# Modulation chunks held back by a tile in the first layer's first expert product, 32 of them from tile 24 on, and eight moved to the second layer's

## The chip, the cores and the metric

The kernel runs on one core of a Trainium2 chip. The metric is device time in microseconds (us) of one execution; the time before is 1799.27 us, the median of 3 runs from 1798.03 to 1800.52 us.

## The reference

A decoder trunk of two layers on 256 tokens of width 1024, all in float32. What matters here is the modulation by a conditioning vector `c`, of which each layer needs six groups of 1024 numbers, and the expert stage (PEER):

```python
mod = (c_act @ w_ada + b_ada)[:, None, :]
sh1, sc1, g1, sh2, sc2, g2 = jnp.split(mod, 6, axis=-1)
h = rms_norm(x, norm1_g) * (1 + sc1) + sh1
...
x = x + g1 * (merged @ w_out)
h2 = rms_norm(x, norm2_g) * (1 + sc2) + sh2
x = x + g2 * peer_ffn(h2, peer_wq, peer_sub_keys, peer_down, peer_up)
```

In `peer_ffn` each token picks 16 of 16384 experts for each of 8 heads, and computes the sum of `gate * gelu(h2 . down[expert]) * up[expert]`.

## The kernel before, in words

The kernel computes the expert stage densely: a **first product** of all 256 tokens with all of `down`, in 128 tiles of 128 experts, then gelu and a mask of gates, then a **second product** with `up`, again in 128 tiles. The matrices stream from HBM in transfers of 512 KB (128 x 1024 float32).

The work before an expert stage (mixing, queries, scores) is the same in both layers. Two stretches between stages, the bridges, apply the updates and the norm.

**The stream.** `Src.seq` lists every matrix of the program in order. `dma_ahead` (line 170) issues their transfers on SP's queue into a ring of 5 buffers, `raw`; a transfer waits until the buffer's last reader is done. `cast_step` (line 207) takes the next entry. A matrix is split for TensorE into `hi` (line 232, ACT) and `lo` (line 225, DVE), 3 buffers each, at raised priority, so that two tiles stand ready ahead of the one that PE multiplies. `chunk_mm` multiplies a tile: 8 times the three matmuls of lines 303 to 305.

**Modulation chunks.** 128 of the modulation's numbers take one 512 KB transfer of `w_ada` and a multiply with a sum on DVE (`ada_chunk`, lines 188 to 205). They are mixed into the stream. `ada(layer, groups)` lists them by groups of 8 chunks, and `mix(a, b, first, last)` spreads the chunks `b` over the entries `first` to `last` of `a`. In the first layer's first product there are 40: its own last group and four of the second layer's. In that product the conditioning vector stands in two PSUM banks, and a chunk is two instructions of 512 columns each (line 193): one sums into `mod`, one into `halves`. Its second product has 16 more, with the vector in SBUF (`cb`). The second layer's products have none.

**Between the tiles.** In the first third of a first product DVE still does the top-k work of the retrieval (`run_fill`). Then the gates come in, four tokens at a time: POOL makes one-hots (line 918, 4 an item), DVE others (lines 921 and 923), PE multiplies them, and DVE multiplies the gates into the activations (`gate_use`, line 939), for the columns that are there; ACT copies the others (line 942). `act_use` (line 971) multiplies gelu values in. Each second tile, ACT writes `ungated` values to HBM (lines 949 and 950), and SP copies rows of `up` (line 951).

A scheduler with a cost model of its own sets the order in which the instructions stand on each engine, within priorities; on the chip each engine then takes its instructions in that order and waits at each for what it needs. `tc.keep_in_program_order(op)` adds an edge of order: the instruction stays behind the one of its engine that was written just before it.

Of the kernel before, what the change touches and what calls it, by code (L numbers as in the profile page):

```python
# [9 lines left out]
F32 = mybir.dt.float32  # L10
# [4 lines left out]
OP = mybir.AluOpType  # L15
# [43 lines left out]
def hybrid_trunk(ctx: ExitStack, tc: tile.TileContext, x_in, c_in, vec_in, w_ada, w_in, w_out, w_pq,  # L59
# [103 lines left out]
    class Src:  # L163
# [2 lines left out]
        loaded = 0  # L166
        cast = 0
        seq = []

    def dma_ahead(upto):  # L170
        while Src.loaded < min(upto, len(Src.seq)):
# [16 lines left out]
    def ada_chunk(layer, col, raw):  # L188
        sides = Src.c if isinstance(Src.c, list) else [Src.c]
        w = D // len(sides)  # L190
        for k, (c, m) in enumerate(zip(sides, (mods[layer], halves))):
            v = raw[:, k * w:(k + 1) * w]
            nc.vector.scalar_tensor_tensor(v, v, 1.0, c, op0=OP.mult, op1=OP.mult, accum_out=m[:, col:col + 1])  # L193
        n = 8
        if layer == 0 and col < G1:
            n = 1
        if (col + 1) % n == 0:
            lo = col + 1 - n
            m = mods[layer][:, lo:lo + n]
            if len(sides) > 1:  # L200
                nc.vector.tensor_add(m, m, halves[:, lo:lo + n])
            nc.vector.tensor_add(m, m, vec[:, layer, V_ADA + lo:V_ADA + lo + n])
            if lo // 8 in (SC1 // 8, SC2 // 8):
                at = lo % 8 + (V_N1 if lo // 8 == SC1 // 8 else V_N2)
                nc.vector.scalar_tensor_tensor(m, m, 1.0, vec[:, layer, at:at + n], op0=OP.add, op1=OP.mult)

    def cast_step(late=None):
        k = Src.cast
        if k >= len(Src.seq):
            return False  # L210
        dma_ahead(k + 1)
        kind, _, arg = Src.seq[k]
        raw = raws.pop(k)
        Src.cast += 1
        if kind == "ada":
            ada_chunk(arg[0], arg[1], raw)
        elif kind in ("whole", "early"):
            ready.append((raw, None))
        else:
            hi = stream.tile([P, D], F32R, name="hi", tag="hi", bufs=3)  # L220
            lo = stream.tile([P, D], F32R, name="lo", tag="lo", bufs=3)

            def low():
                if arg is None:
                    nc.vector.tensor_sub(lo, raw, hi.bitcast(F32))  # L225
                else:
                    nc.vector.scalar_tensor_tensor(lo, raw, arg, hi.bitcast(F32), op0=OP.mult,
                                                   op1=OP.subtract)

            with tc.high_priority(offset=AHEAD):  # L230
                if arg is None:
                    nc.scalar.copy(hi, raw)  # L232
                else:
                    nc.scalar.activation(hi, raw, AF.Copy, scale=arg)
                if late is None:
                    low()
                else:
                    late.append(low)
            ready.append((hi, lo))
        dma_ahead(k + RAW)  # L240
        return True

# [12 lines left out]
    def ada(layer, groups):  # L255
        return [("ada", w_ada[layer, p], (layer, p)) for g in groups for p in range(8 * g, 8 * g + 8)]
# [15 lines left out]
    for layer in range(DEPTH):  # L272
# [15 lines left out]
        dn = mats(down, layer, 128)  # L288
        ups = [("whole" if n // 2 in WHOLE_UP[layer] else "mat", up[layer, n], None) for n in range(128)]
        if layer + 1 < DEPTH:  # L290
            dn = mix(dn, ada(0, [5]) + ada(1, range(4)), 4, 112)
            ups = mix(ups, ada(1, [4, 5]), 6, 120)
        seq += dn + ups
    Src.seq = seq
    dma_ahead(RAW)
# [610 lines left out]
    def experts(layer, rest):  # L906
# [195 lines left out]
                turn(1, 1, high)  # L1102
            return low + high, qg

        if layer + 1 < DEPTH:
            Src.c = [bank("acc", 4) for _ in range(2)]
            for k, half in enumerate(Src.c):
                nc.scalar.copy(half, cact[:, k * 512:(k + 1) * 512])
        gdone = 0
        made = 0  # L1110
        waiting = []
# [138 lines left out]
```

## Time and profile before

| | |
|---|---|
| median of 3 runs | 1799.27 us |
| profiled execution | 1804.13 us, span 1802.4 us |
| first layer's first product, tile 0 to tile 127 | 188.67 to 617.31 us |
| second layer's first product, tile 0 to tile 127 | 1092.32 to 1488.19 us |
| DVE's waits for chunk transfers, whole span | 57.3 us |

The stages are told apart by counting the matmuls of line 303: 8 for each tile. The profile shows, for a stretch, how long each engine was busy, and for each wait what ended it. Engines issue in order, so an instruction that waits holds all that stands behind it on its engine.

### The profile page before, as it was taken

Reading aid. Unit: us, or ns where it says so; the run is one execution under the profiler, and the core shown is the slowest. Engines: PE = TensorE matmul, PEld = TensorE weight load, DVE = VectorE, ACT = ScalarE, POOL = GpSimd, SP = SyncE. Lnnn points to the kernel's source line nnn. Section 1 sums busy time; section 2 is a strip of 40 time slices with the busy share of each in tenths; the row PEclk is TensorE's granted clock in tenths of the full one; section 3 lists DMA queues with packets and bytes.
Section 4 is the critical chain, followed back from the end, with each engine's and each line's share of the span. In section 5 each row is a group of like instructions: output and inputs, shape, how many; then the busy total and the mean of one; then the engine's idle time right before and its main releaser. Section 6 shows DMA issues by size and latency. Waiting matters only on the chain. (4 is left out here: it accounts for less than half of the span.)

```text
span 1802.4 us, 34404 instructions
## 1 busy us (share of the span) xinstructions
PE 1736.8 (96%) x12504; PEld 1599.5 (89%) x12504; DVE 1515.8 (84%) x3465; ACT 913.6 (51%) x1419; POOL 907.5 (50%) x826
## 2 busy tenths in 40 slices
PE   7999999999999999999999999999999999999998
PEld 6789899998988988888889999999999998888886
DVE  5858998878888789999987589967778877999998
ACT  2446455544444554445556664555555546444543
POOL 1000101577879556657620002037999973777672
PEclk9999999999999999999999999999999999999999
DMA  9965798888887789999974456988787778999995
GB/s 366 312 231 173 227 299 287 280 254 269 268 257 247 237 313 328 334 346 344 341 255 141 146 171 212 294 287 247 248 255 245 237 234 283 360 354 349 350 351 206
DMA packets 189867, 492.83 MB, mean 273 GB/s; under 512 B 19521, under 2 KB 85441, under 8 KB 188546
## 3 DMA queue, kind: packets, MB, share of 16 engines
q1 hardware_dynamic: 134752, 405.33, 67.4%
q0 software_dynamic: 19984, 68.44, 10.4%
q10 hardware_dynamic: 34962, 16.88, 3.2%
q8 instruction: 98, 1.61, 0.4%
q14 instruction: 71, 0.58, 0.1%
HBM read 470.64 MB, written 61.87 MB: 295 GB/s over the span
## 5 line engine op out<-in xcount | busy, mean ns | idle before, releaser
L232 ACT CAST hi<-raw 128x1024 fp32r<-128x1024 f32 x538 | 564.5, 1050 | 616.7 <-PE ch L305 265.9
L225 DVE TENSOR_TENSOR lo<-raw,hi 128x1024 fp32r<-128x1024 f32 x538 | 660.4, 1228 | 118.6 <-ACT hi L232 117.1
L304 PE MATMUL ch<-hh,lo 128*128 128x256 f32 x2336 | 655.2, 281 | 15.5 <-DVE lo L225 15.5
L303 PE MATMUL ch<-hh,hi 128*128 128x256 f32 x2336 | 660.3, 283 | 5.9 <-ACT ungated L949 5.8
L305 PE MATMUL ch<-hh,hi 128*128 128x256 f32 x2336 | 651.6, 279 | 0.0
L918 POOL TENSOR_SCALAR oh<-iota,picks 128x128 f16<-128x128 f16 x512 | 498.4, 991 | 235.4 <-DVE arena L833 67.4
L1008 POOL DMA_INDIRECT arena<-rows,arena x256 | 371.2, 1450 | 221.1 <-DVE arena L1019 113.3
L304 PEld LDWEIGHTS ch<-hh,lo 128*128 128x128 f32 x2336 | 443.5, 190 | 18.8 <-DVE lo L225 18.4
L303 PEld LDWEIGHTS ch<-hh,hi 128*128 128x128 f32 x2336 | 441.9, 189 | 7.1 <-ACT ungated L949 6.6
L305 PEld LDWEIGHTS ch<-hh,hi 128*128 128x128 f32 x2336 | 441.8, 189 | 0.0
L1028 PE MATMUL acc<-hi,hh 128*128 128x512 f32 (+2 forms) x1920 | 419.5, 359 | 2.8 <-DVE hh L986 2.4
L1028 PEld LDWEIGHTS acc<-hi,hh 128*128 128x128 f32 x1920 | 339.4, 188 | 49.3 <-DVE hh L986 6.4
L1028 PE MATMUL acc<-lo,hh 128*128 128x512 f32 x960 | 230.9, 361 | 2.8 <-DVE lo L225 2.7
L1028 PEld LDWEIGHTS acc<-lo,hh 128*128 128x128 f32 x960 | 172.7, 188 | 27.7 <-DVE lo L225 5.1
L1019 DVE SCALAR_TENSOR_TENSOR arena<-arena 128x256 f32<-128x256 f32 (+1 forms) x254 | 140.2, 552 | 9.1
L942 ACT ACTIVATE arena<-g 128x240 f32<-128x240 f32 (+35 forms) x128 | 41.5, 324 | 117.0 <-DVE arena L939 108.1
L779 POOL CAST arena<-arena 128x512 f16<-128x512 uint32 x32 | 26.3, 835 | 147.7 <-DVE arena L768 119.2
L923 DVE TENSOR_TENSOR oh<-oh,parts 128x512 f16<-128x512 f16 x256 | 99.9, 432 | 0.0
L193 DVE SCALAR_TENSOR_TENSOR raw<-raw,acc 128x512 f32<-128x512 f32 x80 | 51.8, 683 | 47.8 <-DMA raw<-in_w_ada 47.8
L931 PE MATMUL g<-oh 128*128 128x128 f16 x512 | 76.3, 222 | 13.9 <-POOL oh L918 9.6
L1014 DVE SCALAR_TENSOR_TENSOR arena<-arena,chosen,ident 128x128 f32<-128x128 f32 x256 | 88.6, 346 | 0.0
L921 DVE TENSOR_TENSOR oh<-iota,parts 128x512 f16<-128x512 f16 x128 | 56.6, 443 | 27.5 <-POOL oh L918 15.0
(231 smaller groups left out, 1788.4 us busy)
## 6 DMA issues: line engine op xcount, KB each, us to landing
raw<-in_down SPq DMA_DIRECT2D x256, 512.0 KB, 4.4
raw<-in_up SPq DMA_DIRECT2D x256, 512.0 KB, 5.2
raw<-in_w_ada SPq DMA_DIRECT2D x96, 512.0 KB, 5.1
rows<-in_up SPq DMA_DIRECT2D x64, 384.0 KB, 5.1
raw<-in_w_pq SPq DMA_DIRECT2D x32, 512.0 KB, 3.7
rows<-in_up SPq DMA_DIRECT2D x64, 256.0 KB, 5.1
rows<-ungated ACTq DMA_DIRECT2D x128, 128.0 KB, 4.5
raw<-in_w_in SPq DMA_DIRECT2D x26, 512.0 KB, 4.4
```

Source lines behind the costliest of these rows:

```text
L225: nc.vector.tensor_sub(lo, raw, hi.bitcast(F32))
L232: nc.scalar.copy(hi, raw)
L303: nc.tensor.matmul(dst, hi[:, cols], k[0], start=start, stop=False, **kw)
L304: nc.tensor.matmul(dst, lo[:, cols], k[0], start=False, stop=False, **kw)
L305: nc.tensor.matmul(dst, hi[:, cols], k[1], start=False, stop=stop, **kw)
L918: nc.gpsimd.tensor_scalar(oh[:, i, :], iota, picks[:, t:t + 1], None, op0=OP.is_equal)
L923: nc.vector.tensor_tensor(og[j], on, wide(1 + j), op=OP.mult)
L931: nc.tensor.matmul(dst, oh[:, i, :], og[0][:, i // 2, :, i % 2], start=True, stop=False)
L1008: nc.gpsimd.indirect_dma_start(out=ring[:, k % RING, :], out_offset=None, in_=rows[layer][:, :], in_offset=bass.IndirectOffsetOnAxis(ap=wh ...
L1014: nc.vector.scalar_tensor_tensor(v[:, wide:], v[:, wide:], chosen[:, 1, k:k + 1], ident, op0=OP.mult, op1=OP.mult, accum_out=w8[:, k:k + 1])
L1019: nc.vector.scalar_tensor_tensor(total, v[:, :wide], w8[:, k:k + 1], total, op0=OP.mult, op1=OP.add)
L1028: nc.tensor.matmul(acc[piece][:, :hi - lo], w[:, t * P:(t + 1) * P], u[:, lo:hi], start=piece not in opened, stop=last, skip_group_check=True)
```

## The change

Four edits:

- In `cast_step` a chunk that comes while the vector is in PSUM isn't computed at once. It is put into `Src.held`, and computed when the next matrix has been split.
- The first half of each such chunk (into `mod`) is kept in program order, that is behind that split's `lo`. The second half (into `halves`) is not.
- The first layer's first product gets 32 chunks, spread from tile 24 to 124, instead of 40 from tile 4 to 112. One group of eight, group 5 of the second layer, moves to the second layer's first product, tiles 40 to 120. The second product keeps 16 (groups 3 and 4 instead of 4 and 5).
- For that, the second layer loads the vector again (a transfer on POOL's queue into `cb`) and copies it to two PSUM banks, as the first layer does.

```diff
+        held = []
...
-            nc.vector.scalar_tensor_tensor(v, v, 1.0, c, op0=OP.mult, op1=OP.mult, accum_out=m[:, col:col + 1])
+            op = nc.vector.scalar_tensor_tensor(v, v, 1.0, c, op0=OP.mult, op1=OP.mult, accum_out=m[:, col:col + 1])
+            if len(sides) > 1 and k == 0:
+                tc.keep_in_program_order(op)
...
-        if kind == "ada":
+        if kind == "ada" and isinstance(Src.c, list):
+            Src.held.append((arg[0], arg[1], raw))
+        elif kind == "ada":
             ada_chunk(arg[0], arg[1], raw)
...
             ready.append((hi, lo))
+            while Src.held:
+                ada_chunk(*Src.held.pop(0))
         dma_ahead(k + RAW)
...
         if layer + 1 < DEPTH:
-            dn = mix(dn, ada(0, [5]) + ada(1, range(4)), 4, 112)
-            ups = mix(ups, ada(1, [4, 5]), 6, 120)
+            dn = mix(dn, ada(0, [5]) + ada(1, range(3)), 24, 124)
+            ups = mix(ups, ada(1, [3, 4]), 6, 120)
+        else:
+            dn = mix(dn, ada(1, [5]), 40, 120)
...
-        if layer + 1 < DEPTH:
-            Src.c = [bank("acc", 4) for _ in range(2)]
-            for k, half in enumerate(Src.c):
-                nc.scalar.copy(half, cact[:, k * 512:(k + 1) * 512])
+        c = cact
+        if layer:
+            c = work.tile([P, D], F32, name="cb", tag="oh", bufs=2)
+            nc.gpsimd.dma_start(c, bass.AP(tensor=c_dram.tensor, offset=c_dram.offset, ap=[[0, P], [1, D]]))
+        Src.c = [bank("acc", 4) for _ in range(2)]
+        for k, half in enumerate(Src.c):
+            nc.scalar.copy(half, c[:, k * 512:(k + 1) * 512])
```

DVE before, in the first layer's first product, where the gates have come in. `raw_4359` is a chunk (`mod1` and `halves` are the sums of its halves, `acc` the vector in PSUM); `lo<-raw,hi` are splits of matrices, in the stream's order 4162, 4231, 4273, 4321, with 4162 five transfers ahead of the chunk on SP.

```order
L225 TENSOR_TENSOR lo_4318<-raw_4162,hi_4317 128x1024
L939 SCALAR_TENSOR_TENSOR arena_93<-arena_93,g_4300 128x60x4
L923 TENSOR_TENSOR oh_4309<-oh_4309,parts_96 128x512 x2
L193 SCALAR_TENSOR_TENSOR raw_4359,mod1_108<-raw_4359,acc_1623 128x512
L193 SCALAR_TENSOR_TENSOR raw_4359,halves_106<-raw_4359,acc_1624 128x512
L225 TENSOR_TENSOR lo_4362<-raw_4231,hi_4361 128x1024
L971 TENSOR_TENSOR arena_93<-arena_93,gt_4350 128x2x60
L921 TENSOR_TENSOR oh_4401<-iota2_87,parts_96 128x512
L939 SCALAR_TENSOR_TENSOR arena_93<-arena_93,g_4392 128x62x4
L921 TENSOR_TENSOR oh_4418<-iota2_87,parts_96 128x512
L923 TENSOR_TENSOR oh_4401<-oh_4401,parts_96 128x512 x2
L939 SCALAR_TENSOR_TENSOR arena_93<-arena_93,g_4409 128x62x4
```

Both halves stand ahead of the splits of three matrices that SP fetches before the chunk (4231 here, 4273 and 4321 in the rows that follow).

DVE in the changed kernel, at a like place. `raw_4694` is the chunk, `raw_4518` the one before it; the matrices are 4482, 4526, 4591, 4633 in the stream's order, with 4482 five transfers ahead of the chunk.

```order
L230 TENSOR_TENSOR lo_4630<-raw_4482,hi_4629 128x1024
L980 TENSOR_TENSOR arena_93<-arena_93,gt_4622 128x2x80
L930 TENSOR_TENSOR oh_4669<-iota2_87,parts_96 128x512
L948 SCALAR_TENSOR_TENSOR arena_93<-arena_93,g_4660 128x68x4
L230 TENSOR_TENSOR lo_4697<-raw_4526,hi_4696 128x1024
L930 TENSOR_TENSOR oh_4686<-iota2_87,parts_96 128x512
L932 TENSOR_TENSOR oh_4669<-oh_4669,parts_96 128x512 x2
L194 SCALAR_TENSOR_TENSOR raw_4518,mod1_108<-raw_4518,acc_1623 128x512
L948 SCALAR_TENSOR_TENSOR arena_93<-arena_93,g_4677 128x68x4
L194 SCALAR_TENSOR_TENSOR raw_4694,halves_106<-raw_4694,acc_1624 128x512
L932 TENSOR_TENSOR oh_4686<-oh_4686,parts_96 128x512 x2
L230 TENSOR_TENSOR lo_4741<-raw_4591,hi_4740 128x1024
```

The `halves` half stands ahead of two such splits (4591 and 4633). The `mod1` half comes later:

```order
L930 TENSOR_TENSOR oh_4780<-iota2_87,parts_96 128x512
L948 SCALAR_TENSOR_TENSOR arena_93<-arena_93,g_4771 128x70x4
L230 TENSOR_TENSOR lo_4789<-raw_4633,hi_4788 128x1024
L932 TENSOR_TENSOR oh_4780<-oh_4780,parts_96 128x512 x2
L230 TENSOR_TENSOR lo_4831<-raw_4702,hi_4830 128x1024
L194 SCALAR_TENSOR_TENSOR raw_4694,mod1_108<-raw_4694,acc_1623 128x512
L980 TENSOR_TENSOR arena_93<-arena_93,gt_4821 128x2x92
```

It stands behind the split of 4702, the matrix that SP fetches just after the chunk; so the chunk's buffer is read until there.

DVE of the changed kernel in the second layer's first product, at the first of the eight new chunks, `raw_13805`. The split of `raw_13581` frees the buffer that its transfer takes.

```order
L230 TENSOR_TENSOR lo_13762<-raw_13581,hi_13761 128x1024
L230 TENSOR_TENSOR lo_13802<-raw_13621,hi_13801 128x1024
L980 TENSOR_TENSOR arena_93<-arena_93,gt_13794 128x2x4
L194 SCALAR_TENSOR_TENSOR raw_13805,halves_106<-raw_13805,acc_12043 128x512
L930 TENSOR_TENSOR oh_13841<-iota2_87,parts_96 128x512
L948 SCALAR_TENSOR_TENSOR arena_93<-arena_93,g_13832 128x44x4
L930 TENSOR_TENSOR oh_13858<-iota2_87,parts_96 128x512
L948 SCALAR_TENSOR_TENSOR arena_93<-arena_93,g_13849 128x44x4
L932 TENSOR_TENSOR oh_13841<-oh_13841,parts_96 128x512
L230 TENSOR_TENSOR lo_13867<-raw_13656,hi_13866 128x1024
L932 TENSOR_TENSOR oh_13841<-oh_13841,parts_96 128x512
L932 TENSOR_TENSOR oh_13858<-oh_13858,parts_96 128x512 x2
```

The `halves` half stands ahead of three splits of matrices that SP fetches before the chunk (13656, 13718 and 13765).

ACT in the bridge ahead of the second layer's retrieval, before:

```order
L318 ACTIVATE rn_11486<-g_11429,eps_82 128x2
L353 ACTIVATE hh_94<-arena_93,mod1_108 128x256 x8
L413 COPY arena_93<-g_11491 128x256
L415 COPY shift_11494<-ch_11427 128x1
L415 COPY shift_11494<-ch_11428 128x1
```

and in the changed kernel:

```order
L327 ACTIVATE rn_11452<-g_11395,eps_82 128x2
L362 ACTIVATE hh_94<-arena_93,mod1_108 128x256 x2
L1120 COPY acc_12042<-cb_12040 128x512
L1120 COPY acc_12043<-cb_12040 128x512
L362 ACTIVATE hh_94<-arena_93,mod1_108 128x256 x6
L422 COPY arena_93<-g_11457 128x256
L424 COPY shift_11460<-ch_11393 128x1
```

The two copies of the vector to PSUM stand among the shifts, behind the second of eight.

## Rows read from the trace of the kernel before

**Rows 1.** The profile page: the span, and part 1, busy time of the engines.

```profile
span 1802.4 us, 34404 instructions
...
PE 1736.8 (96%) x12504; PEld 1599.5 (89%) x12504; DVE 1515.8 (84%) x3465; ACT 913.6 (51%) x1419; POOL 907.5 (50%) x826
```

**Rows 2.** Busy time of each engine in six stretches (the view by windows; the columns are those of its head line). The first three are the first layer's first product, cut at the first matmul of tiles 0, 24, 48 and 127; the last three are the same cuts of the second layer's.

```profile
core 0: us, PE busy (x) PEld busy (x) DVE busy (x) ACT busy (x) POOL busy (x), PEclk, DMA share, GB/s
188.67:263.74 75.07, 68.54 (x587) 67.03 (x585) 70.46 (x291) 36.93 (x51) 8.27 (x12) 1.00 0.85 271
263.74:341.44 77.70, 73.29 (x614) 72.43 (x615) 68.14 (x155) 41.59 (x63) 18.92 (x23) 0.96 0.89 295
341.44:617.31 275.87, 258.62 (x2377) 250.29 (x2377) 225.71 (x453) 131.80 (x257) 215.66 (x235) 0.99 0.81 255
1092.32:1162.54 70.22, 68.40 (x587) 68.14 (x586) 70.19 (x299) 37.65 (x52) 9.19 (x12) 0.98 0.84 260
1162.54:1231.25 68.71, 68.71 (x617) 68.58 (x616) 47.56 (x73) 40.24 (x62) 24.69 (x22) 1.00 0.89 285
1231.25:1488.19 256.94, 251.44 (x2377) 246.62 (x2377) 200.73 (x354) 132.40 (x257) 239.70 (x235) 1.00 0.78 244
```

**Rows 3.** The first of these stretches, line 303 alone (first column PE's matmuls, 8 a tile of the product: 192 are 24 tiles).

```profile
188.67:263.74 75.07, 53.03 (x192) 35.91 (x192) 1.00 0.85 271
```

**Rows 4.** The same for line 193 on DVE: the modulation chunks (4 rows a chunk: two halves, and a read of the accumulator for each).

```profile
188.67:263.74 75.07, 10.39 (x32) 1.00 0.85 271
263.74:341.44 77.70, 11.82 (x38) 0.96 0.89 295
341.44:617.31 275.87, 29.98 (x92) 0.99 0.81 255
```

**Rows 5.** Who waited for whom from 341.44 to 617.31 us (tiles 48 to 127 of the first layer's product): us in total, times, longest.

```profile
DVE raw L193 <- DMA raw<-in_w_ada: 38.9, 21, 4.2
...
ACT arena L942 <- DVE arena L939: 89.6, 45, 5.8
...
PE ch L304 <- DVE lo L225: 8.6, 8, 2.3
```

**Rows 6.** The same from 188.67 to 341.44 us (tiles 0 to 47).

```profile
DVE raw L193 <- DMA raw<-in_w_ada: 8.9, 9, 1.9
...
ACT ungated L949 <- DMA rows<-ungated: 16.2, 11, 3.7
...
PE ch L303 <- ACT ungated L949: 5.8, 3, 3.5
```

**Rows 7.** The timeline around one chunk, engine by engine (start, us, engine, line, operation, tiles, count, and in brackets the idle time before and what ended it): SP's transfers, then DVE, ACT and PE.

```profile
408.12 0.33 SPq L175 DMA_DIRECT2D raw<-in_w_ada  x1
...
414.56 2.81 SPq L175 DMA_DIRECT2D raw<-in_down  x2
...
406.88 1.21 DVE L225 TENSOR_TENSOR lo<-raw,hi 128x1024 fp32r<-128x1024 f32 x1
...
409.89 0.29 DVE L971 TENSOR_TENSOR arena<-arena,gt 128x144 f32<-128x144 f32 x1
413.23 0.69 DVE L193 SCALAR_TENSOR_TENSOR raw<-raw,acc 128x512 f32<-128x512 f32 x1 [3.04 <-DMA raw<-in_w_ada]
...
413.84 0.68 DVE L193 SCALAR_TENSOR_TENSOR raw<-raw,acc 128x512 f32<-128x512 f32 x1
...
414.45 0.42 DVE L921 TENSOR_TENSOR oh<-iota,parts 128x512 f16<-128x512 f16 x1
...
415.80 1.22 DVE L225 TENSOR_TENSOR lo<-raw,hi 128x1024 fp32r<-128x1024 f32 x1
...
415.30 0.38 ACT L942 ACTIVATE arena<-g 128x248 f32<-128x248 f32 x1 [4.63 <-DVE arena L939]
...
417.07 0.38 PE L304 MATMUL ch<-hh,lo 128*128 128x256 f32 x1 [1.65 <-DVE lo L225]
```

**Rows 8.** Three short stretches of the first layer's product around a stop of PE, by windows (columns as in the second group).

```profile
295.00:300.00 5.00, 1.52 (x14) 1.32 (x12) 5.00 (x12) 4.94 (x8) 4.31 (x5) 0.92 0.66 208
300.00:306.80 6.80, 6.75 (x34) 6.75 (x35) 5.73 (x14) 2.27 (x3) 0.00 (x0) 0.56 0.84 271
306.80:312.00 5.20, 5.20 (x47) 5.20 (x46) 2.71 (x4) 2.15 (x4) 0.00 (x0) 1.00 0.90 291
```

**Rows 9.** Transfers issued from 188 to 618 us: engine, count, KB each, median us from issue to landing.

```profile
raw<-in_down SPq DMA_DIRECT2D x122, 512.0 KB, 4.6
raw<-in_w_ada SPq DMA_DIRECT2D x40, 512.0 KB, 4.9
```

**Rows 10.** ACT's timeline in the stretch between mixing and retrieval, first layer (with the two copies of the conditioning vector to PSUM) and second layer (without).

```profile
142.45 0.91 ACT L353 ACTIVATE hh<-arena,mod 128x256 fp32r<-128x256 f32 x2 [1.67 <-DVE arena L351]
143.27 1.09 ACT L1108 COPY acc<-arena 128x512 f32<-128x512 f32 x2
...
150.87 0.50 ACT L875 ACTIVATE arena<-arena,shift 128x256 f32<-128x256 f32 x1
...
1046.39 0.91 ACT L353 ACTIVATE hh<-arena,mod 128x256 fp32r<-128x256 f32 x2 [1.67 <-DVE arena L351]
...
1054.53 0.50 ACT L875 ACTIVATE arena<-arena,shift 128x256 f32<-128x256 f32 x1
```

**Rows 11.** The chain that ended last, one piece in the second layer's second product (start, us, what).

```profile
1558.32 9.57 DMA raw<-in_up
```

## The prediction

> **What bounds the kernel now.** I began with the page [rows 1]: PE is busy for 96% of the span and DVE for 84%. That says little here, since matmuls overlap and the share is a mean over stages. So I cut the two layers' first products into equal stretches of tiles [rows 2, 3]. Both layers run the same matmuls on the same 128 tiles; the first layer also has 40 modulation chunks in it, the second none. The three stretches (tiles 0 to 23, 24 to 47, 48 to 126) take 75.07, 77.70 and 275.87 us in the first layer, and 70.22, 68.71 and 256.94 us in the second [rows 2]. The differences are 4.9, 9.0 and 18.9 us, 32.8 us together. That is what the chunks, and whatever else differs, cost now, and it bounds what the change can give in the first layer.
>
> Next I asked what ends the waits there. In tiles 48 to 126, DVE waits 38.9 us in 21 waits for a chunk's transfer, and ACT waits 89.6 us for DVE's gate multiply, line 939 [rows 5]. The timeline of one chunk shows the chain [rows 7]. DVE ends a split (lo, line 225) at 408.09, and the chunk's transfer is issued at 408.12: it had waited for the buffer which that split read last. DVE reaches the chunk at 410.18 and stands still for 3.04 us until the transfer lands. Behind it stand the gate multiply, for which ACT idles 4.63 us, and the next split, which ends at 417.02; PE, which waits for that split, starts again at 417.07 after 1.65 us. So the order on DVE asks for the chunk too soon after its buffer is free: 23 chunks [rows 4] cost this stretch 18.9 us.
>
> Why does one chunk cost PE only 18.9 / 23 = 0.82 us? Because DVE has room. In the second layer it idles 256.94 - 200.73 = 56.2 us in 79 tiles [rows 2], 0.71 us a tile. The first layer has a chunk per 79 / 23 = 3.4 tiles, so 2.4 us of room for each. A chunk takes 29.98 / 23 = 1.30 us of work [rows 4] and 38.9 / 23 = 1.69 us of waiting [rows 5], 2.99 us in all. The excess of 0.6 us is near the 0.82 us seen.
>
> In tiles 0 to 47 the waits for chunks are small, 8.9 us [rows 6]; the transfers there hold DMA at 0.85 to 0.89 busy [rows 2], and ACT waits 16.2 us for its own write of ungated values, at most 3.7 us at once [rows 6]. One such stop reaches PE: from 295 to 300 us it issues 14 matmuls, against 47 in 5.2 us later, and then 6.8 us run at a mean granted clock of 0.56, most of them at 1.2 GHz instead of 2.4, with 34 matmuls [rows 8]. At 9 a microsecond the stop costs about 3.4 us and the low clock about 3.0 us.
>
> **Tiles 0 to 23: no chunk.** Eight chunks (32 rows) go: 10.39 us of DVE work [rows 4] and part of the 8.9 us of waits. The second layer without chunks is 4.9 us faster. I take -4 us. Bounds: 0, if the first layer's start is slow for another reason, and -6.4 us, if the pace becomes that of the second layer's next 24 tiles (68.71).
>
> **Tiles 24 to 47: 7 chunks instead of 9.5.** By the table, 32 chunks over 100 tiles make 7 by tile 47. Saved are 2.5 x 1.30 = 3.3 us of DVE work, and some of the 6.4 us of the stop and its clock. But the stretch stays full: the chunks still load DMA, which is at 0.89. Bounds: 0 and -9.0 us (the second layer's pace). I take -4 us, between them, since fewer transfers help, but nothing in the change makes the write of ungated values land sooner.
>
> **Tiles 48 to 126: 25 chunks instead of 23, later on DVE.** The order shows that the pinned half of a chunk now stands behind one later split, so it cannot wait. The other half isn't pinned: it still stands ahead of two earlier splits, where both halves stood ahead of three. What counts is DVE's work between the split that frees the buffer (five transfers back on SP) and the first half. Before, for the chunk shown, it was a gate multiply and two one-hot products, about 3 x 0.42 = 1.3 us [rows 7]. Now it is a whole split (1.21), five one-hot or gate operations and one more gate multiply (0.42 each), a multiply by the gelu (0.29) and the previous chunk's pinned half (0.61 from start to start), about 4.6 us [rows 7]; a landing takes 4.9 us [rows 9]. So the wait falls from 1.69 to some 0.3 to 0.5 us, and the chunk to about 1.8 us, within 79 / 25 x 0.71 = 2.2 us of room. By room alone the stretch would reach the second layer's pace, -18.9 us. By proportion it would keep 25 x 0.82 x 1.8 / 2.99 = 12.3 us of the 18.9, a gain of 6.6 us. The middle is 12.8; I take -12 us. Bounds: 0 and -18.9 us.
>
> What is late next is POOL, whose one-hots the gate matmuls need. It takes 235 of them in either layer, 215.66 us here (0.92 each) and 239.70 us there (1.02 each), 93% of that stretch [rows 2]: so 256.94 us is a floor, whatever DVE does. POOL is slower where DVE runs denser, though no chunk is there. The Trainium skill (SBUF — State Buffer, Who interferes with whom) says that a DVE instruction with two SBUF inputs contends with GpSimd's reads, and one with at most one SBUF input does not. The trace agrees as far as it goes: chunks, whose second input is in PSUM, stand beside the faster one-hots, and by that rule DVE's splits, packed closer after the change, would slow POOL. By that rule alone the sum would be -4 us instead of -16; the POOL rival below works that case out from rows.
>
> **The second layer: 8 chunks more.** Work 8 x 1.30 = 10.4 us, in a stretch with 0.71 x 10 = 7.1 us of room per chunk. Their free half stands ahead of three splits, directly behind the split after the one that frees the buffer: one tile, 68.71 / 24 = 2.86 us [rows 2], against a landing of 4.9 us [rows 9], so DVE waits some 2 us each. By room that costs nothing; at the first layer's 0.82 us it is 6.6 us. I take +3.7 us, bounds 0 and +10. The conditioning vector comes by one more POOL transfer, queued ahead of the row gathers of the first layer's second product, which its table asks for from tile 12 on: nothing. Its two copies to PSUM (1.09 us) come among ACT's shifts of the bridge. The first layer has the same copies there: from the first shift to the second use of the product it takes 150.87 - 142.45 = 8.42 us, the second layer without them 1054.53 - 1046.39 = 8.14 us [rows 10]. I take +0.3 us. Chunks of the second product stay 16: nothing.
>
> **Sum.** -4 - 4 - 12 + 3.7 + 0.3 = -16 us. The profiled execution took 1804.13 us, 4.9 above the median of 1799.27 us; on it the sum gives 1788.1, and I give it on the median: **1783.3 us**, said as 1783.
>
> **Rivals.**
> - *The first layer takes the second's pace.* All of -4.9 - 9.0 - 18.9, with +3.5 in the second layer: 1770 us. For it: DVE's room. Against: DMA stays loaded, and 32 chunks stay.
> - *The free half undoes it.* If landings lengthen to 6 or 7 us, the half at its early place waits as long as before, for 25 chunks and 8 more. Then -4 - 2 - 6 + 7: 1794 us. For it: that half is not pinned, and a transfer now leaves later, since the chunk's buffer is held two splits longer.
> - *POOL becomes the bound.* One-hots at 1.10 us make 235 x 1.10 = 258.5 us; with the 17.2 us that POOL idles in the second layer's stretch, 275.7: no gain in tiles 48 to 126, 1795 us.
> - *Slower: the held buffer starves the splits.* With five buffers and one held, the matrix five transfers behind a chunk leaves only when the pinned half has run. Its split is due three tiles later, 8.6 us, and less the split, the half and the cast before it (1.21 + 0.61 + 1.05) 5.7 us are left; two tiles split ahead let PE feel it only some 2.9 us later. So it decides from landings of 8.6 us on. A row shows one of 9.57 us, in the second product [rows 11]. At that size 32 chunks cost 1.0 us each, +32 us, in place of the gains behind tile 24: 1799 - 4 - 16 + 32 + 4 = 1815 us. Against it: the medians of 4.6 and 4.9 us in this stretch [rows 9], and no wait of ACT's casts for a matrix among its longest there.
>
> **Chances.** A measurement can tell about 0.2%, 3.6 us, from no change: faster is below 1795.7, slower above 1802.9. The forecast (1776 to 1790) has 0.48, the second layer's pace 0.18, the free half 0.15, POOL 0.10, the starved splits 0.09. Of the free half and POOL about a third each falls within 0.2% (0.09). So faster 0.82, same 0.09, slower 0.09. The range runs from 1768, the second layer's pace and a little of the better bound of the first stretch, to 1799, which holds the two rivals of a lost gain and leaves out the slower one.
>
> **What would show it.** DVE's wait for the chunks' transfers, 38.9 us in the long stretch, should be below 15 us, and ACT's wait for the gate multiply below 50. The three stretches should take about 71, 74 and 264 us, the second layer's tiles 48 to 126 about 261 us. The forecast is wrong if that wait stays above 30 us, if a cast waits for its matrix in tiles 24 to 126, or if POOL's one-hots there pass 1.08 us.

## The result, and the profile after

| | before | changed |
|---|---|---|
| median, measured together | 1802.11 us (6 runs, 1798.03 to 1807.79) | 1780.9 us (6 runs, 1777.25 to 1787.06) |
| ratio, 95% interval | | 0.9892, 0.9873 to 0.9912 |
| profiled execution | 1804.13 us | 1781.52 us, span 1779.7 us |

The change is faster by 1.1%, some 21 us. The page shows no engine with less work to do; the span is shorter around the same 12504 matmuls, which keep PE busy for 8 us less (answers to [rows 1]):

```profile
span 1779.7 us, 34446 instructions
...
PE 1728.6 (97%) x12504; PEld 1595.0 (90%) x12504; DVE 1516.9 (85%) x3465; ACT 916.7 (52%) x1421; POOL 915.5 (51%) x827
```

The same six stretches as in [rows 2], cut at tiles 0, 24, 48 and 127 of the first and then the second layer's first product:

```profile
186.32:257.16 70.84, 68.29 (x587) 67.57 (x586) 69.32 (x295) 37.73 (x52) 9.19 (x12) 1.00 0.76 238
257.16:329.75 72.59, 70.80 (x617) 69.99 (x616) 54.75 (x102) 38.94 (x61) 23.61 (x24) 1.00 0.86 286
329.75:589.43 259.68, 252.67 (x2379) 248.10 (x2378) 231.34 (x465) 133.20 (x258) 219.69 (x235) 0.99 0.85 273
1069.38:1139.52 70.14, 68.32 (x587) 68.07 (x586) 70.11 (x299) 38.05 (x52) 9.19 (x12) 0.98 0.83 260
1139.52:1209.28 69.76, 68.90 (x617) 68.65 (x615) 46.66 (x75) 40.48 (x62) 22.96 (x22) 1.00 0.87 273
1209.28:1465.28 256.00, 251.07 (x2379) 246.37 (x2378) 211.55 (x386) 133.47 (x257) 237.44 (x235) 1.00 0.81 263
```

The long stretch of the first layer fell by 16.2 us although DVE is busy there for 5.6 us more. The chunks in these stretches, as in [rows 4] (now line 194, four rows a chunk; the last row is the second layer's long stretch):

```profile
257.16:329.75 72.59, 10.31 (x30) 1.00 0.86 286
329.75:589.43 259.68, 33.71 (x98) 0.99 0.85 273
...
1209.28:1465.28 256.00, 10.36 (x30) 1.00 0.81 263
```

The waits from 329.75 to 589.43 us, which answer to [rows 5] (us in total, times, longest; line 951 was 942, line 948 was 939, line 313 was 304):

```profile
ACT arena L951 <- DVE arena L948: 58.6, 44, 5.0
...
DVE raw L194 <- DMA raw<-in_w_ada: 19.4, 15, 3.4
...
PE ch L313 <- DVE lo L230: 1.3, 1, 1.3
```

DVE stands half as long before a chunk, 19.4 us instead of 38.9, ACT waits 31 us less for the gate multiply behind it, and PE's waits for a split fall from 8.6 to 1.3 us. The transfers of `w_ada` land only 0.3 us sooner there (count, KB, median us from issue to landing; before, then changed):

```profile
raw<-in_w_ada SPq DMA_DIRECT2D x22, 512.0 KB, 4.8
raw<-in_w_ada SPq DMA_DIRECT2D x24, 512.0 KB, 4.5
```

The wait of a chunk fell by 0.9 us, from 1.69 to 0.79 us: for the most part it is that more work stands ahead of the instruction that needs the transfer.

One place got slower. From the first matmul of tile 127 to the first of the second layer's first product before took 1092.32 - 617.31 = 475.0 us [rows 2], and now 1069.38 - 589.43 = 479.95 us. Nearly all of it is lost at the step to the second product: counted from the first matmul of tile 127, PE comes to its 95th after 17.1 us before, and after 21.8 now. The waits of PE from 589.4 to 616 us of the changed kernel:

```profile
PE acc L1037 <- ACT hh L994: 2.1, 1, 2.1
...
PE acc L1037 <- DVE hh L995: 0.6, 1, 0.6
```

Before, PE waits for nothing in this place. The timeline shows what is ahead of it: ACT stands 3.42 us for its own write of ungated values, behind it stands the cast of a matrix, behind that the casts of `hh` which PE needs.

```profile
591.98 0.38 ACT L958 ACTIVATE ungated<-ch 128x256 f32<-128x256 f32 x1 [3.42 <-DMA rows<-ungated]
592.85 1.04 ACT L237 CAST hi<-raw 128x1024 fp32r<-128x1024 f32 x1 [0.49 <-PE ch L314]
593.80 2.08 ACT L994 CAST hh<-arena 128x512 fp32r<-128x512 f32 x3
...
594.47 0.73 PE L1037 MATMUL acc<-hi,hh 128*128 128x512 f32 x2 [2.05 <-ACT hh L994]
```

### The profile page after: what moved, and what is told of

Read it like the earlier page. It is cut to its first block, busy times and chain, and to the rows that moved or that the text cites. A ratio compares the mean times of both kernels' runs of the same rounds, so it can differ in the third digit from the quotient of the medians.

```text
span 1779.7 us, 34446 instructions
## 1 busy us (share of the span) xinstructions
PE 1728.6 (97%) x12504; PEld 1595.0 (90%) x12504; DVE 1516.9 (85%) x3465; ACT 916.7 (52%) x1421; POOL 915.5 (51%) x827
```

## The experiments

Ten kernels ran, in three groups. Each group has its own runs of the kernel before (medians 1801.22, 1800.56 and 1798.78 us), and ratios are to these. **Theory:** what the chunks cost is DVE standing still for a chunk's matrix with splits queued behind it; the hold takes it away where it reaches. **Rivals:** the gain comes of the table (fewer chunks, thinner spread), or of DVE's work as such. In the texts that were on record before each run, theory A and theory B are those of that run alone. The table collects all kernels; the columns are the median, the ratio with its interval, DVE's waits for chunks in tiles 48 to 126, and three stretches of the profiled execution (tiles 0 to 47; 48 to 126; tile 127 to the second layer's first product). The profiled execution is one of the runs, and some lie off the median: 1790.31 us with the hold alone, 1796.41 with the spread alone and 1788.68 with the vector in SBUF, so the stretches of the first two look too good and those of the third too long.

| kernel | us | ratio | chunk waits | 0–47 | 48–126 | step on |
|---|---|---|---|---|---|---|
| before | 1802.1 | 1 | 38.9 (21) | 152.8 | 275.9 | 475.0 |
| changed | 1780.9 | 0.9892 (0.9873–0.9912) | 19.4 (15) | 143.4 | 259.7 | 479.9 |
| hold only | 1794.2 | 0.9971 (0.9956–0.9986) | 26.2 (15) | 147.3 | 267.6 | 476.4 |
| spread only | 1801.0 | 1.0003 (0.9989–1.0018) | 41.7 (24) | 146.8 | 274.8 | 475.5 |
| both halves pinned | 1776.3 | 0.9864 (0.9842–0.9885) | none | 138.3 | 254.3 | 480.4 |
| vector loaded later | 1781.2 | 0.9892 (0.9872–0.9912) | 23.2 (17) | 143.7 | 258.4 | 478.1 |
| pinned, vector later | 1771.4 | 0.9837 (0.9818–0.9857) | none | 139.6 | 254.9 | 476.6 |
| the same, vector in SBUF | 1785.9 | 0.9919 (0.9897–0.9942) | none | 139.4 | 271.8 | 477.4 |
| changed, end at tile 116 | 1780.7 | 0.9904 (0.9880–0.9928) | 27.4 (20) | 141.5 | 265.7 | 475.0 |
| pinned, old table | 1781.5 | 0.9897 (0.9878–0.9917) | none | 148.2 | 255.5 | 475.4 |
| pinned, vector later, end 116 | 1772.5 | 0.9858 (0.9835–0.9880) | none | 139.8 | 254.8 | 474.4 |
| pinned, vector later, extra work | 1787.9 | 0.9939 (0.9918–0.9960) | none | 140.8 | 264.3 | 479.6 |

### The two halves of the change apart

The hold and the pin with the table of before (so the second layer has no chunks here and doesn't load the vector again):

```diff
-            dn = mix(dn, ada(0, [5]) + ada(1, range(3)), 24, 124)
-            ups = mix(ups, ada(1, [3, 4]), 6, 120)
-        else:
-            dn = mix(dn, ada(1, [5]), 40, 120)
+            dn = mix(dn, ada(0, [5]) + ada(1, range(4)), 4, 112)
+            ups = mix(ups, ada(1, [4, 5]), 6, 120)
```

> The changed kernel with the table of before: all 40 chunks in the first layer's first product from tile 4 to 112, none in the second layer's, groups 4 and 5 in the second product; the holding back and the pin stay. Theory A (what the change gains behind tile 24 comes from where a chunk stands on DVE): tiles 48 to 126 take about 262 us instead of 275.9, DVE's wait for the chunks there falls from 38.9 to about 20 us, tiles 0 to 23 stay at 74 to 75 us since their 8 chunks stay, the step to the second product is as before; in all some 15 to 17 us less than before, ratio 0.991. Theory B (fewer and later chunks gain it): tiles 48 to 126 stay above 270 us, ratio 0.997 or more.

And the new table without hold or pin:

```diff
-            if len(sides) > 1 and k == 0:
-                tc.keep_in_program_order(op)
...
-        if kind == "ada" and isinstance(Src.c, list):
+        if False:
```

> The changed kernel's table (32 chunks from tile 24 on, 8 in the second layer's first product) without the holding back and without the pin; both halves of a chunk then stand ahead of three earlier splits, as in most of before. Theory A: tiles 0 to 23 take 71 us, but tiles 48 to 126 keep about 275 us, and the second layer pays 0.8 us for each of its 8 chunks, 6 us; with the 5 us at the step to the second product the total is within 5 us of before, ratio 0.998 to 1.003. Theory B: about the time of the changed kernel, ratio 0.989.

The spread alone gives nothing by its runs, 1.0003, as theory A has it. But the hold alone gives 5 us, where theory A wanted 16: its ratio is that of theory B, and its 267.6 us from tile 48 on lie between the two. Tiles 0 to 23 took 71.9 us with their 8 chunks, where I expected 74 to 75. Neither half makes the 21 us; together they do. The chunk rows of the waits in tiles 48 to 126 tell why, of the hold alone:

```profile
DVE raw L194 <- DMA raw<-in_w_ada: 26.2, 15, 3.5
```

and of the spread alone:

```profile
DVE raw L194 <- DMA raw<-in_w_ada: 41.7, 24, 3.9
```

So, without the hold a thinner spread leaves every chunk as early as it was, and DVE waits as before. With the hold the free half still waits, and there the spread counts: 26.2 us with a chunk per 2.7 tiles, 27.4 with one per 2.9 (the end at tile 116, below), 19.4 and 23.2 us with one per 3.1 (changed kernel, and the one with the vector loaded later). The rest of the table's part lies in tiles 0 to 47: 147.3 against 143.4 us.

### The free half pinned too

```diff
-            if len(sides) > 1 and k == 0:
+            if len(sides) > 1:
```

> The changed kernel with the second half of a chunk pinned too, so that both halves stand behind one later split. If the free half is what still waits (theory A), DVE's wait for chunks falls from 19.4 to under 3 us in tiles 48 to 126; by DVE's room this stretch then gains little, 259.7 to some 257 us, since the second layer's 256 us is POOL's floor, and the total is 2 to 4 us below the changed kernel, ratio 0.987. If the cost of a chunk were in proportion to its work and waits, the stretch would gain as much as the wait that goes, more than 5 us.

The time is 1776.3 us, about 5 us below the changed kernel by the ratios, whose intervals overlap a little. The stretch from tile 48 on, and all of DVE's waits in it:

```profile
326.43:580.71 254.28, 250.54 (x2378) 246.22 (x2377) 232.12 (x463) 132.54 (x256) 233.81 (x236) 1.00 0.87 279
```

```profile
DVE lo L230 <- ACT hi L237: 13.6, 21, 1.5
DVE oh L930 <- POOL oh L927: 5.0, 7, 1.0
DVE oh L930 <- PE g L941: 3.2, 6, 0.8
DVE oh L930 <- issue: 0.6, 2, 0.4
```

No row of the chunks is left. With the same 25 chunks (32.3 us of DVE's work) the stretch takes 254.28 us, less than the second layer's took before with none, 256.94 us [rows 2]. So where no chunk waits, the chunks cost nothing that shows against a stretch without any; the first layer's own stretch without chunks was not run. The stretch fell by 5.4 us, twice what I expected, to below the 256 us that I had called POOL's floor: POOL's one-hots take 233.81 us here, 239.70 in the second layer [rows 2]. Over all kernels the stretch follows that wait: 38.9 and 41.7 us go with 275.9 and 274.8, 26.2 and 27.4 with 267.6 and 265.7, 19.4 and 23.2 with 259.7 and 258.4, none with 254.3 to 255.5 (the two kernels below with other or more work of DVE apart).

### Both pinned, with the table of before

The table's lines are those of the first experiment.

> The table of the kernel before (40 chunks from tile 4 to 112, none in the second layer's first product), with both halves of each chunk held and pinned behind the next split. Theory A (the table matters only through the half that still waits; with both pinned no chunk waits, whatever the table): no wait of the chunks for their matrix in tiles 4 to 126; tiles 48 to 126 take 253 to 257 us as with the new table, tiles 0 to 47 lose 2 to 5 us to their 17 chunks against 8: 1776 to 1781 us, ratio 0.986 to 0.989. Theory B (the work of 40 chunks in 108 tiles, 24 early tiles among them, is too much beside the splits, held or not; the spread is needed for its own sake): near the kernel that holds with the old table, 1789 to 1794 us, ratio 0.993 to 0.997.

1781.5 us: theory A's mechanism (no chunk waits, 255.5 us in tiles 48 to 126), just above its time. This is the cleanest comparison of all: the table, the 40 chunks and the second layer are those of before, and the order on DVE alone takes the long stretch from 275.9 to 255.5 us and some 19 us off the whole. The table is then worth 5 to 6 us, and not where the waits were: tiles 0 to 47 take 148.2 us against 138.3 with the new table, a loss of 10 where I expected 2 to 5; the step on to the second layer takes 5 us less. PE's waits in tiles 0 to 47 of this kernel follow; with both halves pinned and the new table the first row is absent:

```profile
PE ch L310 <- ACT ungated L956: 6.1, 5, 2.7
PE ch L311 <- DVE lo L230: 1.9, 1, 1.9
PE g L938 <- POOL oh L925: 0.8, 1, 0.8
```

This is the stop of [rows 6, 8]: ACT stands for its write of ungated values, 26.2 us in 15 waits against 14.2 in 9 with the new table, and PE behind it. Why the write lands later is not shown: DMA's busy share in tiles 0 to 47 is 0.86 against 0.85.

### Where the 5 us of the step come from

First, the vector of the second layer, which the changed kernel loads at 580.1 us, loaded 400 us later, in the second layer's mixing (986.4 us):

```diff
+                if layer:
+                    Src.cb = work.tile([P, D], F32, name="cb", tag="oh", bufs=2)
+                    tc.keep_in_program_order(nc.gpsimd.dma_start(Src.cb, ...))
...
-            c = work.tile([P, D], F32, name="cb", tag="oh", bufs=2)
-            nc.gpsimd.dma_start(c, ...)
+            c = Src.cb
```

> The changed kernel with the second layer's load of the conditioning vector issued behind the load of the keys in the second layer's mixing, instead of right at the step to the first layer's second product. Theory A (that transfer, 512 KB beside the one for the second product, delays the stream there: landings of 7.5 to 10.5 us, ACT's wait of 3.4 us): from tile 127 of the first product to the second product's 94th matmul the time falls from 26.7 us to before's 21.9, and the total is 4 to 5 us below the changed kernel, ratio 0.9865. Rival (the chunks' end at tile 124 or the two PSUM banks held until then delay the step): nothing changes there.

1781.2 us, no gain in the time; the stretch from tile 127 on is 1.8 us shorter in the profiled execution, all of it at the step (20.0 us to the 95th matmul, where the changed kernel takes 21.8). The transfer alone doesn't explain the step. Second, the chunks end at tile 116 instead of 124:

```diff
-            dn = mix(dn, ada(0, [5]) + ada(1, range(3)), 24, 124)
+            dn = mix(dn, ada(0, [5]) + ada(1, range(3)), 24, 116)
```

> The changed kernel with the 32 chunks of the first layer's first product on tiles 24 to 116 instead of 24 to 124. Theory A (the 5 us lost at the step to the second product come of held chunks in the last tiles, whose late multiplies and late free buffers push the last splits): from tile 127 to the second layer's product 475 to 477 us instead of 480; the denser chunks cost 1 to 2 us in tiles 48 to 126: 1776 to 1779 us, ratio 0.986 to 0.988. Theory B (the step loses them because the faster product leaves its transfers behind at the end, wherever the chunks stand): 479 to 481 us there, and 1781 to 1783 us in all, ratio 0.989 to 0.990.

The place is found: 475.0 us from tile 127 on, 17.3 of them to the 95th matmul, with the vector's load still where the changed kernel has it. In this kernel's last tiles ACT's wait is

```profile
ACT ungated L958 <- DMA rows<-ungated: 0.6, 1, 0.6
```

instead of 3.4 us, and the first six transfers for the second product land in 5.5 us by the median where the changed kernel's take 8.4 (issues in tiles 48 to 126; engine, count, KB, us), here of the changed kernel

```profile
raw<-in_up SPq DMA_DIRECT2D x6, 512.0 KB, 8.4
```

and here with the end at tile 116:

```profile
raw<-in_up SPq DMA_DIRECT2D x6, 512.0 KB, 5.5
```

The 95 matmuls tell the parts. They take 17.1 us before, with the hold alone, with the spread alone (whose chunks end at 124 as well, with the vector's load at the step) and with both halves pinned on the old table. With held chunks up to 124 they take 21.8 us (changed) and 22.1 (both halves pinned) with the load at the step, and 20.0, 19.3 and 19.0 us with the load later (alone, with the pin, and with the vector in SBUF). So it takes the hold and chunks that reach the last tiles, and the load is worth 1.8 to 2.8 of the 4.7 to 5.0 us. One kernel does not fit: with the extra work, below, held chunks up to 124 and the later load, they take 17.3 us. But the time with the end at 116 did not fall as theory A had it: the free halves wait longer in the denser table, and tiles 48 to 126 grew by the 6 us that the step gave back. Why a held chunk near the end makes these transfers late is not settled.

### Both edits together, and the end at 116 with them

In the texts that follow, the early vector is the later load of the experiment above: early in the second layer, not at the step ahead of it.

> The changed kernel with two edits at once: the second half of each chunk is pinned behind the next split too, and the second layer's conditioning vector is loaded during its keys' mixing instead of at the step to the second product. Theory A (DVE's wait for a chunk's matrix, with splits queued behind it, is all that the table and the pins act on): with both halves pinned the wait row of the chunks is absent from tiles 48 to 126, that stretch takes 253 to 256 us, and the early vector takes about 2 us from the step to the second product (480 to 478 us from tile 127 to the second layer's product): 1774 to 1776 us, ratio 0.985 to 0.986. Theory B (the vector's load is hidden at the step): nothing from it, 1776 to 1778 us, ratio 0.986 to 0.987.

1771.4 us, ratio 0.9837: the fastest kernel here, a bit below theory A's 1774. The way from tile 127 to the second layer is shorter by 3.8 us than with both halves pinned alone, 2.8 us of that at the step. With the end at tile 116 in addition:

> Both halves pinned, the early vector, and the 32 chunks on tiles 24 to 116 instead of 24 to 124. Theory A (denser chunks cost only through halves that wait, and none waits here; the step to the second product loses time to held chunks in the last tiles): tiles 48 to 126 stay at 254 to 256 us, where the changed kernel with this end had 265.7 with a waiting half; from tile 127 to the second layer's product 475 us as with the other kernels that end by tile 116: 1769 to 1771 us, ratio 0.983 to 0.984. Theory B (denser chunks cost by DVE's work in itself): tiles 48 to 126 take 258 to 262 us and the time is 1773 to 1778 us, ratio 0.985 to 0.988.

The stretch stays at 254.8 us, as theory A has it: without a waiting half the denser table costs nothing there. The step takes 474.4 us. The time, 1772.5 us, is a little above theory A's 1769 to 1771, and not better than without this edit (ratios 0.9858 and 0.9837, whose intervals overlap).

### More work on DVE, without a wait

The first half's multiply of each chunk is done once more, into a spare sum:

```diff
-                ada_chunk(*Src.held.pop(0))
+                layer_, col_, held_ = Src.held.pop(0)
+                ada_chunk(layer_, col_, held_)
+                v = held_[:, :512]
+                tc.keep_in_program_order(nc.vector.scalar_tensor_tensor(
+                    v, v, 1.0, Src.c[0], op0=OP.mult, op1=OP.mult, accum_out=spare_sum))
```

> Both halves pinned and the early vector, and the first half's multiply of every chunk is done once more into a spare sum, pinned behind the second half: some 25 x (0.68 + 0.08) = 19 us more of DVE in tiles 48 to 126, which raises its busy time there from 231.8 to about 251 us of 254.9. Theory A (what DVE works on a chunk is hidden as long as it doesn't wait; PE sets the stretch): 255 to 260 us there, and in all 0 to 8 us above the kernel without the repeat, ratio 0.984 to 0.988. Theory B (DVE's work on the chunks is on the path, and the change gains because it spreads it thinner): the stretch grows by most of the 19 us to 270 us or more, and with tiles 24 to 47 and the second layer's eight chunks the time by 20 to 30 us, ratio 0.995 to 1.0.

Neither theory has it by the time. The long stretch without the repeat and with it, and PE's waits in the latter:

```profile
328.18:583.05 254.87, 251.26 (x2379) 247.07 (x2378) 231.81 (x463) 132.66 (x256) 232.03 (x235) 1.00 0.86 277
329.37:593.68 264.31, 259.41 (x2379) 255.19 (x2378) 247.76 (x516) 132.47 (x258) 221.66 (x235) 0.99 0.85 271
```

```profile
PE ch L317 <- ACT ungated L967: 4.1, 2, 2.6
PE g L949 <- POOL oh L936: 0.7, 1, 0.7
```

DVE is busy for 16 us more, and the stretch takes 9.4 us more. PE's idle time rises by only 1.3 us (4.9 against 3.6), though two stops behind ACT's writes are new; the other 8.2 us lie in PE's busy time, 259.41 against 251.26 us for the same matmuls. Most of that is not the repeat's doing. In tiles 24 to 38 of the second layer's first product no chunk stands in either kernel, and yet the same 374 matmuls, without a gap, take longer in the kernel with the repeat (the second line):

```profile
1129.94:1172.12 42.18, 42.18 (x374) 42.13 (x373) 31.67 (x47) 25.31 (x37) 15.72 (x12) 1.00 0.90 291
1143.26:1186.88 43.62, 43.62 (x374) 43.56 (x373) 31.46 (x47) 25.44 (x37) 14.48 (x12) 1.00 0.86 281
```

These 15 tiles take 1.44 us more. At that rate, by an estimate, 79 tiles take 7.6 us more, and without it the stretch would take 256.7 us, inside theory A's 255 to 260. So the kernel runs 16 to 18 us behind the one without the repeat, but it doesn't show that the extra work costs them: its matmuls have a slower pace where nothing was added, and no run here shows why. What the repeat itself costs stays open; in the long stretch it is some 2 us by the estimate.

### The vector in SBUF

In the first layer the chunks' factor is read from SBUF instead of two PSUM banks. By then other values have taken the vector's place there, so this kernel is read for its time alone.

```diff
-        Src.c = [bank("acc", 4) for _ in range(2)]
-        for k, half in enumerate(Src.c):
-            nc.scalar.copy(half, c[:, k * 512:(k + 1) * 512])
+        if layer:
+            ...
+        else:
+            Src.c = [c[:, k * 512:(k + 1) * 512] for k in range(2)]
```

> As the kernel with both edits, but in the first layer the chunks' second factor is read from SBUF instead of from PSUM, so that 64 multiplies of DVE have two SBUF inputs. Theory A (POOL's one-hots are slowed by how densely DVE runs at all, not by where the second input lies): POOL's one-hots in tiles 48 to 126 stay at 0.98 to 1.02 us each, 232 to 238 us in sum, and the stretch stays at 253 to 257 us; the time is within 2 us of the kernel with both edits. Theory B (the rule of the Trainium skill, page SBUF - State Buffer, Who interferes with whom: a DVE instruction with two SBUF inputs contends with GpSimd): about 50 multiplies of 0.64 to 0.68 us each slow POOL while they run; if POOL's work doubles for those 33 us its sum rises by some 16 us to 250 us, it is late for the gate matmuls, and the stretch takes 258 to 265 us.

Theory B, and more. POOL's one-hots in tiles 48 to 126 (count, busy us, mean ns, idle before), with the vector in PSUM:

```profile
L931 POOL TENSOR_SCALAR oh<-iota,picks 128x128 f16<-128x128 f16 x234 | 231.6, 1009 | 12.0 <-issue 9.3 <-POOL oh L931 2.5
```

and in SBUF, with PE's waits of the stretch:

```profile
L931 POOL TENSOR_SCALAR oh<-iota,picks 128x128 f16<-128x128 f16 x235 | 252.0, 1091 | 9.5 <-issue 9.5
```

```profile
PE g L944 <- POOL oh L931: 12.9, 25, 1.6
```

The same one-hots take some 20 us more beside 34.6 us of such multiplies, PE waits for them 25 times, and the stretch takes 271.79 us instead of 254.87. The Trainium skill (SBUF — State Buffer, Who interferes with whom) says that a DVE instruction with two SBUF inputs contends with GpSimd's reads and one with at most one, outside DVE's 2-port modes, does not; the trace agrees, 1091 ns a one-hot against 1009. Against 1771.4 us with the vector in PSUM, the edit costs 14.5 of the 29 us that kernel gained.

## Why the prediction was right

The forecast was 1783 us (1768 to 1799); the median is 1780.9. Its sum was -16 us; the profiled executions differ by 22.6. The terms:

- **Tiles 0 to 23: -4, measured -4.2** (75.07 to 70.84 us). Right in size, and the spread-only kernel has 70.0 us there. But the hold alone, with the eight chunks still there, has 71.9, so taking them out is not the only way to this gain.
- **Tiles 24 to 47: -4, measured -5.1.** Near, but not by shorter waits for chunks: these rose there, from 0.7 to 2.0 us a wait (before, then changed):

```profile
DVE raw L193 <- DMA raw<-in_w_ada: 4.3, 6, 1.8
DVE raw L194 <- DMA raw<-in_w_ada: 14.0, 7, 3.4
```

What went is the stop of [rows 8], of which the prediction counted "some": PE's wait behind ACT's write, in these tiles of the kernel before

```profile
PE ch L303 <- ACT ungated L949: 4.0, 2, 3.5
```

is absent in the changed kernel, and the mean granted clock is 1.00 where it was 0.96 [rows 2]. It is absent with the spread alone too, and there with the hold alone (3.6 us), so it goes with the table. The write itself lands no sooner, as argued: in tiles 0 to 47 ACT's row fell from 16.2 [rows 6] to

```profile
ACT ungated L958 <- DMA rows<-ungated: 9.5, 5, 3.6
```

All of these 9.5 us lie in tiles 24 to 47, where the row had 7.0 before; the fall is that of tiles 0 to 23.
- **Tiles 48 to 126: -12, measured -16.2.** The mechanism was right, the size too small. I took the middle between room and proportion. A chunk now takes 33.71 / 24.5 = 1.38 us and 19.4 / 24.5 = 0.79 us of waiting, 2.17 us in all, just within the 2.2 us of room that I worked out, and the gain is near that of room. The wait itself fell less than I said (to 0.79 us a chunk, not 0.3 to 0.5): I had counted the free half's cover of 4.6 us at one place of the order, and 15 of 24 chunks still wait. So two misses partly cancelled: more waiting was left, and it cost less. Both bounds held for the change. The pinned kernels pass the better one with 254.3 to 255.5 us, so the 256.94 us that the prediction called a floor is none: POOL's one-hots cost less in this stretch than in the second layer's. (That POOL is slower where DVE runs denser holds in those rows only if the chunks are left out of DVE's work; with them DVE is busy for 82% of the first layer's stretch and 78% of the second's.)
- **The second layer's eight chunks: +3.7, measured 0.** Tile 0 to tile 127 takes 395.9 us in both. DVE waits 1.1 us a chunk where I had 2, and each chunk has ten tiles of room; from 1209.28 to 1465.28 us:

```profile
DVE raw L194 <- DMA raw<-in_w_ada: 7.7, 7, 2.0
```

- **The vector's transfer and its copies: +0.3, and "nothing" at the step; measured +4.9.** This step failed: a term put at nothing cost 4.7 us. The transfer is a part of it, 1.8 to 2.8 us where its load was moved, but not by itself: the kernel that ends at tile 116 keeps the transfer and loses 0.2 us. What I left out is that held chunks now reach the last tiles, and that ACT's write of ungated values, which waits for a transfer, stands ahead of the casts for the next product's first matmuls. Behind the step 0.2 us are left, near the +0.3 for the copies.
- **Ahead of the product: 0, measured -2.4** (its start, 188.67 to 186.32 us). No edit lies there; the other kernels start between 186.1 and 189.6 us, so this is the spread between executions.

The base was 1799.27 us; measured beside the changed kernel, before took 1802.11. So the time came out 2.4 us from the forecast, while the gain was 21 us where the sum had 16, and inside the sum two misses cancel, -4.2 us in the long stretch and +4.6 at the step. The mechanism of the long stretch was right; that the time came so close is in part luck.

**The rivals.** The second layer's pace did not come (1770 us), but the kernel with both halves pinned and the vector loaded later has it, at 1771.4. The free half undid part: it keeps 19.4 us of waits, and pinning it is worth 5 us. POOL did not become the bound: 219.69 / 235 = 0.93 us a one-hot, where I had set 1.08 as the limit; that rival's mechanism is real, and appears when the vector moves to SBUF. The held buffer starved the splits only a little. Casts waited for no matrix in the first layer's product before; now they wait 0.7 us in the long stretch, and in tiles 24 to 47

```profile
ACT hi L237 <- DMA raw<-in_down: 3.4, 2, 2.3
```

PE waits 1.8 us for splits in these tiles, 0.8 before, so the loss that this rival foresaw did not come. (Its sum, 1815 us, counts the 16 us of gains that it says are lost; without them it is 1831.)

**What would show it.** Stretches 71, 74 and 264 us: 70.84, 72.59 and 259.68. The second layer's long stretch, forecast at 261, took 256.00. The two waits missed their marks, 19.4 us (below 15) and 58.6 (below 50), though the time came out better. Of the three signs of being wrong one did show, the casts that wait for their matrix behind tile 24: as a sign it was set too sharp, since 4.1 us of such waits came with a gain.

## What to carry to other kernels

Where an engine works in order, a filler that stands ahead of its own data costs by its wait more than by its work: here 30 us of chunk work with 38.9 us of waits cost some 20 us of the long stretch, and 32 us without a wait cost nothing that shows. Put all of its instructions behind the next piece of the main stream by an edge of order, since one that stays free goes back to the early place. Spread fillers more thinly only after that, and read the gain of such an edit stage by stage: the hold and the table gave 5 us and nothing apart and 21 together. Then look at the end of the stage, where the next stage's first transfers meet the last fillers. And where an experiment adds work, look first at a stretch that the work doesn't touch: if that got slower too, the difference is not the work's.

## What was not expected of the hardware

- POOL's 128 x 128 one-hots take 0.94 us by the mean beside DVE waiting for chunks [rows 5] (215.7 us for 234 of them), 1.01 with no chunk waiting, and 0.97 in the kernel with more chunk work, where DVE is busiest but its extra multiplies read PSUM. That fits a price set by what DVE reads from SBUF rather than by how busy it is; only the kernel with the vector in SBUF shows it by itself, with 1.09.
- A stop of PE costs twice: in the long stretch of the kernels before and after, cut into 52 equal pieces, one piece has a granted clock of 0.68 or 0.66, part of it at 1.2 GHz instead of 2.4, right behind a place where PE stood still (for 2.3 us in the changed kernel); in the kernel with both halves pinned and the vector later all 52 are at 1.00.
- Matmuls have more than one pace at a granted clock of 1.00: the same 374 of them, without a gap, took 42.18 us in the changed kernel and in the pinned one with the vector later, and 43.62 us in the one with the extra work. What sets it is open.
